# Two FFN-and-mixer blocks on one core: a bias table written from 128 partitions in four steps, a gain row spread by TensorE, smaller last parts

## Chip, cores and metric

One core of a Trainium2 chip runs the whole program in one launch. The metric is the device time in microseconds (us) of that core; the number that stands for a kernel is the median of its runs.

## The reference, cut

Two blocks of two layers each, over 256 tokens of width 1024 in float32; each layer is an FFN, a mixer and a second FFN of width 2816.

```python
def _rmsnorm(x, gain, eps=1e-6):
    return x * lax.rsqrt(jnp.mean(x * x, -1, keepdims=True) + eps) * gain
def _swiglu(h, w_gate, w_up, w_down):
    return (jax.nn.silu(h @ w_gate) * (h @ w_up)) @ w_down
...
# first block, layer l (the mixer is a convolution with RWKV-7 at l = 0, MLA attention at l = 1)
x = x + 0.5 * _swiglu(_rmsnorm(x, g[0]), ...)
x = x + mix(_rmsnorm(x, g[1]))
x = x + 0.5 * _swiglu(_rmsnorm(x, g[2]), ...)
...
# second block, layer l (the mixer is NSA attention at l = 0, HGRN-2 at l = 1), LN with mean, 1e-5
x = _layer_norm(alpha * x + 0.5 * _swiglu(x, ...), ln_gain[l, 0], ln_bias[l, 0])
x = _layer_norm(alpha * x + mix(x), ln_gain[l, 1], ln_bias[l, 1])
x = _layer_norm(alpha * x + 0.5 * _swiglu(x, ...), ln_gain[l, 2], ln_bias[l, 2])
...
def _rel_bias(table, dist):        # NSA: table is [32 buckets, 16 heads]
    return jnp.moveaxis(table[_t5_bucket(dist)], -1, 0)
```

## The kernel before

x stays in SBUF as two tiles of 128 tokens. Every float32 operand of a product is split into a high part, rounded to the type that TensorE multiplies fast, and a low part, the rest; a product is then three products, high by high, high by low and low by high. Weights are not kept: `weights` (L155) has SyncE load a piece of up to 128 x 2048 numbers, and `hi_lo` (L147) has ScalarE copy the high part (L152) and VectorE subtract the low part (L153), in two halves. Two sets of staging buffers, `st` and `xst`, and of split buffers, `sp` and `xsp`, are used in turn.

An FFN (`_ffn`, L341) walks over units of 256 hidden columns, 11 of them. A unit multiplies x, transposed as `xT`, by its gate and up columns into four rotating PSUM banks (`rot`); ScalarE and VectorE form silu(gate) * up and split it; the down product of the unit before is added to four accumulator banks (`acc`, `down`, L303, products at L181). The last three units' down products come at the end, for token tile 0 and then for token tile 1.

Each engine runs its instructions in one order that a scheduler lays out from the program; SyncE and GpSimd, and in the RWKV mixer ScalarE too (L677), issue DMAs. Work that a later mixer needs ahead of time waits in a list, `K.later`. From unit 4 of an FFN on, one entry of it is taken per unit, issued behind that unit's last multiplication and last activation:

```python
if self.later and u > 3:
    with self.behind_pow(), self.tc.issue_after(self.last_mul), self.tc.issue_after(self.last_act):
        self.later.pop(0)()
```

For NSA the entries are made by `nsa_setup` (L1205). A one-hot product makes the bias by relative distance, 16 heads (partitions) by 384 places, which VectorE copies to `bs` (L1221). It is then needed as `sk`, a DRAM tensor with 128 copies of that table, since the mixer reads it back skewed, each query row shifted by one place (`Gb`, L1280). Six entries, the function `piece`, write it, each 21 or 22 copies by one DMA of GpSimd's queue (L1227). Two further DRAM buffers of the RWKV mixer, `dT`, are filled with zeros by GpSimd's DMAs at the start (L515).

Norms are in `post` (L255). An RMS norm squares two halves with a running sum on ScalarE (L269), then GpSimd adds the halves (L271), multiplies and adds eps (L235) and raises to the power -0.5 (L236); VectorE multiplies x by it and by the gain (L278). Behind it the four halves are transposed on TensorE (L209) and copied and split into `xT` (L213, L214). A layer norm takes its sums with `bn_stats` and `bn_aggr` on VectorE, goes through the same two GpSimd steps, and ends with two VectorE passes (L290, L291). FFN results are added to x at L263.

The program starts (L1843) with SyncE loading x tile 0, then the first gain, spread over 128 partitions by the DMA (512 KB), then x tile 1, and the first weights.

Of the kernel before, what the change touches and what calls it, by code (L numbers as in the profile page):

```python
# [18 lines left out]
P = 128  # L19
# [41 lines left out]
class Core:  # L61
    def __init__(self, tc, ctx):
# [23 lines left out]
        self.second = None  # L86
        self.last_act = None
# [33 lines left out]


# [24 lines left out]
    def hi_lo(self, hi, lo, src):  # L147
# [7 lines left out]
    def weights(self, w, k0, nk, c0, ncols):  # L155
# [11 lines left out]
        self.hi_lo(hi[:, :m], lo[:, :m], st[:, :m])  # L167
        v = lambda a: a[:, :m].rearrange("p (k n) -> p k n", k=nk)
        return v(hi), v(lo)

    def mm3(self, out, terms, start, stop):
# [8 lines left out]
        for i, (a, b) in enumerate(seq):  # L180
            self.last_mm = nc.tensor.matmul(out, a, b, start=start and i == 0, stop=stop and i == n - 1).ins  # L181
# [22 lines left out]
    def transpose_split(self, src, xT, t, k0, nk=4, kind="rot"):  # L204
# [8 lines left out]
        nc.scalar.activation(hi, v, AF.Copy)  # L213
# [6 lines left out]
    def bcast(self, row, n=D, pool=None, tag="gain", bufs=None, queue=None):  # L220
# [8 lines left out]
        return g  # L229

# [24 lines left out]
    def post(self, t, acc, c, alpha=None, rms=None, ln=None, xT=None, out=None):  # L255
# [4 lines left out]
        if acc is not None:  # L260
            for h in range(2):
                s = slice(h * H, (h + 1) * H)
                nc.vector.scalar_tensor_tensor(x[:, s], acc[h], c, x[:, s], ALU.mult, ALU.add)  # L263
        src = [x[:, :H], x[:, H:]]
        if rms is not None:
            ss = self.tmp.tile([P, 4], F32, tag="ss", name=self.n("ss"))
            for h in range(2):
                junk = self.tmp.tile([P, H], F32, tag="xn", name=self.n("junk")) if acc else self.bank("acc")
                nc.scalar.activation(junk, x[:, h * H:(h + 1) * H], AF.Square, accum_out=ss[:, h:h + 1])  # L269
            with self.behind_pow():  # L270
                nc.gpsimd.tensor_tensor(ss[:, 2:3], ss[:, 0:1], ss[:, 1:2], ALU.add)  # L271
            self.rsqrt(ss[:, 3:4], ss[:, 2:3], 1.0 / D, 1e-6)
            yield
            src = []
            for h in range(2):
                s = slice(h * H, (h + 1) * H)
                xn = self.tmp.tile([P, H], F32, tag="xn", name=self.n("xn"))
                self.last_xn = nc.vector.scalar_tensor_tensor(xn, x[:, s], ss[:, 3:4], rms[:, s], ALU.mult, ALU.mult).ins  # L278
                src.append(xn)
            yield  # L280
        if ln is not None:
            st = self.tmp.tile([P, 2, 6], F32, tag="bn", name=self.n("bn"))
            for h in range(2):
                nc.vector.bn_stats(st[:, h, :], x[:, h * H:(h + 1) * H])  # L284
# [18 lines left out]
    def down(self, acc, yT, ws, first, last, toks=(0, 1), halves=(0, 1)):  # L303

        for t in toks:
            for j, (k0, wh, wl) in enumerate(ws):
                for h in halves:
                    s = slice(h * 512, (h + 1) * 512)
                    terms = [(yT[0][:, k0 + k, t * P:(t + 1) * P], yT[1][:, k0 + k, t * P:(t + 1) * P],
                              wh[:, k, s], wl[:, k, s]) for k in range(2)]  # L310
                    self.mm3(acc[t][h], terms, first and j == 0, last and j == len(ws) - 1)
# [21 lines left out]
    def ffn(self, xT, wg, wu, wd, mixed=False):  # L333

        with self.scoped("ff", 2) as self.ff:
# [3 lines left out]
            return self._ffn(xT, wg, wu, wd)  # L339

    def _ffn(self, xT, wg, wu, wd):  # L341
        nc = self.nc
        N = 256
        acc = self.new_acc()
# [49 lines left out]
        for u in range(first, NU):  # L394
# [3 lines left out]
            for w in (wg, wu):  # L398
# [28 lines left out]
        for t in range(2):  # L427
            for (v, y), w in zip(todo, ws):
                self.down(acc, y, [w], False, v == NU - 1, toks=(t,))
# [34 lines left out]
def rwkv_setup(K, p, w, consts):  # L464
# [47 lines left out]
    for s in range(2):  # L512
        ds = [K.dram.tile([8, ITEM], F32, name=f"{name}{s}") for name in ("dA", "dT")]
        for d in ds[1:]:
            nc.gpsimd.dma_start(d[:, :P * P].rearrange("i (p n) -> p i n", n=P),  # L515
                                z[:, :P].rearrange("p (o n) -> p o n", o=1).to_broadcast([P, 8, P]))
# [669 lines left out]
SKN = 6  # L1186
# [19 lines left out]
def nsa_setup(K, pc, w, consts):  # L1206
# [4 lines left out]
    with ExitStack() as ctx:  # L1211
        p = ctx.enter_context(scope)
        rel = p.tile([33, NH], F32, name="rel")
        nc.gpsimd.memset(rel, -1e30)
        nc.gpsimd.dma_start(rel[:32, :], w["rel_bias"])
# [3 lines left out]
        nc.tensor.matmul(bt[:NH, :LR], rel, oh, start=True, stop=True)  # L1219
        bs = p.tile([NH, LR], F32, name="bs")  # L1220
        nc.vector.tensor_copy(bs, bt[:NH, :LR])  # L1221
# [3 lines left out]
    def piece(r0, r1):  # L1225

        nc.gpsimd.dma_start(sk[r0:r1].rearrange("p h l -> h p l"), bs.rearrange("h (o l) -> h o l", o=1).to_broadcast([NH, r1 - r0, LR]))  # L1227
        if r1 == P:
            held.close()

    cuts = [P * n // SKN for n in range(SKN + 1)]
    K.later += [lambda a=a, b=b: piece(a, b) for a, b in zip(cuts, cuts[1:])]
# [593 lines left out]
def program(tc, i, out):  # L1826
    nc = tc.nc
    with ExitStack() as ctx:
# [37 lines left out]
        for l in range(2):  # L1866
# [6 lines left out]
            acc = K.ffn(xT, *ffn2(l, 1))  # L1873
            last = l == 1
            xT = K.after(acc, 0.5, alpha=alpha, ln=ln(l, 2), out=out[0] if last else None, keep_T=not last)
# [36 lines left out]
```

## Time and profile before

| what | value |
|---|---|
| runs shown | 2147.49, 2144.08 and 2138.15 us, median 2144.08 |
| the profiled execution | 2144.05 us, its span 2142.3 us |
| busy share of the span | TensorE 97%, weight loads 83%, VectorE 63%, ScalarE 51%, GpSimd 9% |
| mean granted TensorE clock | 0.992 of full speed |
| DMA | 367 MB, 171 GB/s as a mean over the span |
| first product of the first FFN | 14.62 us after the span's start |

The span is what the profiler saw between the first and the last instruction; the device time has 1.75 us around it. A busy share is a mean over the whole program, so a stretch in which another engine sets the pace shows only in a view of that stretch. A wait row names what the engine waited for last. In the timeline, "x8" means that eight like instructions in a row were joined, and the brackets hold the idle time ahead of them and what ended it. An engine whose name ends in q, as SPq, is issuing (here a DMA), and not computing. [...]

### The profile page before, as it was taken

The numbers are of one execution on the slowest core, as the hardware profiler recorded it, in microseconds if no ns is written. First come the engines' busy times: TensorE is split into PE (matmuls) and PEld (weight loads), VectorE is DVE, ScalarE is ACT, GpSimd is POOL, SyncE is SP. The second block draws the span as 40 slices with busy tenths as digits, with TensorE's granted clock in tenths as the row PEclk, the third lists the DMA queues.
The fourth block names the chain that finished last, engine by engine and source line by source line (L and its number), as shares of the span: only waits on it lengthen the run. The fifth ranks groups of instructions, "written<-read, shape, count | busy, mean of one in ns | idle before, by whom it ended". The sixth has DMA issues, their size and how long they took to land. (4 is left out here: it accounts for less than half of the span.)

```text
span 2142.3 us, 30750 instructions
## 1 busy us (share of the span) xinstructions
PE 2084.4 (97%) x12009; PEld 1788.2 (83%) x12009; DVE 1356.9 (63%) x2316; ACT 1103.1 (51%) x2032; POOL 192.1 (9%) x353
## 2 busy tenths in 40 slices
PE   8999999999999999999997999999999999999998
PEld 6888887788888887888886898788888888987887
DVE  5665764665566567656563667776666666766665
ACT  5554653555455556545453546645545555434553
POOL 2001050000100032000000010100010000241000
PEclk9999999999999999999999999999999999999999
DMA  9653433465566343765558564165546546326551
GB/s 308 213 181 101 130 117 124 169 215 196 169 208 203 131 139 109 250 214 180 156 197 177 188 192 143 41 215 190 190 152 243 185 149 209 126 80 236 189 191 53
DMA packets 257088, 367.27 MB, mean 171 GB/s; under 512 B 6945, under 2 KB 208293, under 8 KB 256944
## 3 DMA queue, kind: packets, MB, share of 16 engines
q1 hardware_dynamic: 249648, 348.48, 49.0%
q0 software_dynamic: 5184, 15.79, 3.4%
q8 instruction: 94, 1.54, 0.3%
q10 hardware_dynamic: 2112, 1.05, 0.2%
q14 instruction: 50, 0.41, 0.1%
HBM read 358.87 MB, written 6.42 MB: 171 GB/s over the span
## 5 line engine op out<-in xcount | busy, mean ns | idle before, releaser
L200 PE MATMUL rot<-xT,sp1h 128*128 128x512 f32 x784 | 196.7, 393 | 0.0
L200 PE MATMUL rot<-xT,sp0h 128*128 128x512 f32 x768 | 193.8, 394 | 1.3 <-DVE xT L214 1.3
L153 DVE TENSOR_TENSOR sp0l<-st,sp0h 128x1024 fp32r<-128x1024 f32 (+4 forms) x126 | 144.5, 1164 | 74.9 <-ACT sp0h L152 74.2
L365 ACT ACTIVATE g<-rot 128x256 f32<-128x256 f32 x296 | 103.9, 377 | 166.9 <-PE rot L202 166.9
L153 DVE TENSOR_TENSOR xsp0l<-xst,xsp0h 128x1024 fp32r<-128x1024 f32 (+4 forms) x106 | 116.9, 1128 | 87.4 <-ACT xsp0h L152 87.2
L366 DVE TENSOR_TENSOR g<-rot,g 128x256 f32<-128x256 f32 x296 | 117.9, 419 | 81.1 <-ACT g L365 80.9
L200 PEld LDWEIGHTS rot<-xT,sp0h 128*128 128x128 f32 x768 | 141.0, 190 | 28.7 <-DVE xT L214 1.7
L200 PEld LDWEIGHTS rot<-xT,sp1h 128*128 128x128 f32 x784 | 142.0, 189 | 26.5
L152 ACT ACTIVATE sp0h<-st 128x1024 fp32r<-128x1024 f32 (+4 forms) x126 | 123.6, 1003 | 62.1 <-PE acc L181 23.1
L153 DVE TENSOR_TENSOR xsp1l<-st,xsp1h 128x1024 fp32r<-128x1024 f32 x80 | 95.7, 1221 | 81.4 <-ACT xsp1h L152 81.4
L153 DVE TENSOR_TENSOR sp1l<-st,sp1h 128x1024 fp32r<-128x1024 f32 (+3 forms) x108 | 122.0, 1148 | 27.8 <-ACT sp1h L152 27.2
L152 ACT ACTIVATE xsp0h<-xst 128x1024 fp32r<-128x1024 f32 (+4 forms) x106 | 100.3, 979 | 70.9 <-DMA xst<-in_ffn_w_gate_dram 58.2
L153 DVE TENSOR_TENSOR sp1l<-xst,sp1h 128x1024 fp32r<-128x1024 f32 x80 | 95.8, 1222 | 60.0 <-ACT sp1h L152 60.0
L417 ACT ACTIVATE hTh<-h 128x256 fp32r<-128x256 f32 x148 | 61.7, 417 | 124.0 <-DVE h L359 124.0
L152 ACT ACTIVATE sp1h<-st 128x1024 fp32r<-128x1024 f32 (+3 forms) x108 | 104.3, 997 | 23.6 <-PE rot L181 7.4
L202 PEld LDWEIGHTS rot<-xT,sp1l 128*128 128x128 f32 x784 | 106.9, 190 | 7.7
L200 PE MATMUL rot<-xT,xsp1h 128*128 128x512 f32 x400 | 102.2, 398 | 10.9 <-ACT xsp1h L152 10.9
L202 PEld LDWEIGHTS rot<-xT,sp0l 128*128 128x128 f32 x768 | 105.0, 190 | 7.8
L152 ACT ACTIVATE xsp1h<-st 128x1024 fp32r<-128x1024 f32 x80 | 82.6, 1052 | 54.9 <-DMA st<-in_ffn_w_gate_dram 32.8
L202 PE MATMUL rot<-xT,sp1l 128*128 128x256 f32 x784 | 109.2, 282 | 0.0
L202 PE MATMUL rot<-xT,sp0l 128*128 128x256 f32 x768 | 107.2, 282 | 0.0
L200 PE MATMUL rot<-xT,xsp0h 128*128 128x512 f32 x416 | 104.6, 393 | 0.0
(570 smaller groups left out, 4922.8 us busy)
## 6 DMA issues: line engine op xcount, KB each, us to landing
st<-in_ffn_w_gate_dram SPq DMA_DIRECT2D x54, 1024.0 KB, 5.2
xst<-in_ffn_w_up_dram SPq DMA_DIRECT2D x48, 1024.0 KB, 5.9
xst<-in_ffn_w_down_dram SPq DMA_DIRECT2D x47, 1024.0 KB, 5.2
st<-in_ffn_w_down_dram SPq DMA_DIRECT2D x41, 1024.0 KB, 4.9
st<-in_ffn_w_up_dram SPq DMA_DIRECT2D x40, 1024.0 KB, 5.3
xst<-in_ffn_w_gate_dram SPq DMA_DIRECT2D x33, 1024.0 KB, 5.2
st<-in_even_w_in_dram SPq DMA_DIRECT2D x12, 1024.0 KB, 5.2
st<-in_hgrn_w_in_dram SPq DMA_DIRECT2D x8, 1024.0 KB, 5.4
```

Source lines behind the costliest of these rows:

```text
L152: self.nc.scalar.activation(hi[:, s], src[:, s], AF.Copy)
L153: self.nc.vector.tensor_sub(lo[:, s], src[:, s], hi[:, s].bitcast(F32))
L200: nc.tensor.matmul(b, wh, both.rearrange("p a n -> p (a n)"), start=i == 0, stop=False, skip_group_check=True)
L202: self.last_mm = nc.tensor.matmul(b[:, :T], wl, xh, start=False, stop=i == n - 1, skip_group_check=True).ins
L365: nc.scalar.activation(g, b[:, T:], AF.Copy)
L366: nc.vector.tensor_add(g, b[:, :T], g)
L417: nc.scalar.activation(y[0][:, i, :], h, AF.Copy)
```

## The change

It has five parts.

1. The bias table is formed on 128 partitions: the table of 16 heads is loaded eight times side by side, so that the one-hot product gives 8 x 16 rows. `sk` is then written by four DMAs of 128 x 4 x 384 numbers, on ScalarE's queue instead of GpSimd's. An empty entry goes ahead of them in `K.later`.
2. The two zero fills of `dT` go from the start of GpSimd's queue into `K.later`, on ScalarE's queue.
3. At the start, the first gain is loaded as one row of 4 KB, ahead of x. `start` issues 14 products of zeros on TensorE and two products of a row of ones by the gain row, which give the gain on all partitions in two accumulator banks, where L278 now reads it. x comes in four loads of 256 KB. The first gate unit's weight copies wait each for one tile's transposed copy (`last_T`) instead of the last normed half (`last_xn`).
4. The squares of an RMS norm are scaled by 1/32 (1/32 squared is 1/1024); eps is added to the first half's sum before the second is there; then come one add and the power. A layer norm's eps is added by VectorE instead of GpSimd.
5. In the last FFN the products of token tile 1 go by output halves, and the very last piece of the second half in two quarters of 256 columns; the final `post` adds the result for that tile in three parts and takes four `bn_stats` of 256.

```diff
+    def start(self, row):
+        nc = self.nc
+        ones = self.gain.tile([P, D], F32, tag="gain", name="ones")[:1, :P]
+        nc.gpsimd.memset(ones, 1.0)
+        idle = self.bank("rot")
+        for _ in range(8):
+            self.zero_bank(idle)
+        out = []
+        for h in range(2):
+            b = self.bank("acc")
+            nc.tensor.matmul(b, ones, row[:, h * 512:(h + 1) * 512], start=True, stop=True)
+            out.append(b)
+        for _ in range(6):
+            self.zero_bank(idle)
+        return out
...
-            self.nc.scalar.activation(hi[:, s], src[:, s], AF.Copy)
+            with self.tc.issue_after(behind[i]) if behind else ExitStack():
+                self.nc.scalar.activation(hi[:, s], src[:, s], AF.Copy)
...
+    def rsqrt_of(self, out, src):
+        self.last_pow = self.nc.gpsimd.tensor_tensor(out, src, self.mhalf, ALU.pow).ins
...
     def post(...)
-            for h in range(2):
-                s = slice(h * H, (h + 1) * H)
-                nc.vector.scalar_tensor_tensor(x[:, s], acc[h], c, x[:, s], ALU.mult, ALU.add)
+            cuts = (0, H, D) if out is None or t == 0 else (0, H, H + H // 2, D)
+            for a, b in zip(cuts, cuts[1:]):
+                s = slice(a, b)
+                nc.vector.scalar_tensor_tensor(x[:, s], acc[a // H][:, a % H:a % H + b - a], c, x[:, s], ...)
...
-                nc.scalar.activation(junk, x[:, h * H:(h + 1) * H], AF.Square, accum_out=ss[:, h:h + 1])
-            with self.behind_pow():
-                nc.gpsimd.tensor_tensor(ss[:, 2:3], ss[:, 0:1], ss[:, 1:2], ALU.add)
-            self.rsqrt(ss[:, 3:4], ss[:, 2:3], 1.0 / D, 1e-6)
+                nc.scalar.activation(junk, x[:, h * H:(h + 1) * H], AF.Square, scale=1.0 / 32, accum_out=...)
+                if h == 0:
+                    with self.behind_pow():
+                        nc.gpsimd.tensor_scalar(ss[:, 2:3], ss[:, 0:1], 1.0, 1e-6, ALU.mult, ALU.add)
+            nc.gpsimd.tensor_tensor(ss[:, 3:4], ss[:, 1:2], ss[:, 2:3], ALU.add)
+            self.rsqrt_of(ss[:, 3:4], ss[:, 3:4])
...
-            self.rsqrt(mv[:, 2:3], mv[:, 1:2], 1.0, 1e-5)
+            nc.vector.tensor_scalar(mv[:, 2:3], mv[:, 1:2], 1e-5, None, ALU.add)
+            self.rsqrt_of(mv[:, 2:3], mv[:, 2:3])
...
     _ffn(...)
-                    with self.tc.issue_after(self.last_xn):
-                        wh, wl = unit(w, u)
+                    wh, wl = self.weights(w, 0, KD, 0, N, behind=self.last_T)
...
+            if not (end and t):
+                for (v, y), w in zip(todo, ws):
+                    self.down(acc, y, [w], False, v == NU - 1, toks=(t,))
+                continue
+            for h in range(2):
+                for (v, y), w in zip(todo, ws):
+                    for q in (range(2) if h and v == NU - 1 else (None,)):
+                        self.down(acc, y, [w], False, v == NU - 1, toks=(t,), halves=(h,), quarter=q)
...
-            nc.gpsimd.dma_start(d[:, :P * P]...)
+        K.later.append(lambda d=ds[1]: nc.scalar.dma_start(d[:, :P * P]...))
...
     nsa_setup
-        rel = p.tile([33, NH], F32, name="rel")
+        rel = p.tile([33, 8, NH], F32, name="rel")
...
-        nc.tensor.matmul(bt[:NH, :LR], rel, oh, start=True, stop=True)
+        nc.tensor.matmul(bt[:, :LR], rel.rearrange("b r h -> b (r h)"), oh, start=True, stop=True)
...
-        nc.gpsimd.dma_start(sk[r0:r1].rearrange("p h l -> h p l"), bs...to_broadcast([NH, r1 - r0, LR]))
+        m = P // 8 // SKN
+        v = sk.rearrange("(k r) h l -> (r h) k l", r=8)[:, n * m:(n + 1) * m, :]
+        nc.scalar.dma_start(v, bs.to_broadcast([P, m, LR]))
...
+    K.later += [lambda: None] + [lambda n=n: piece(n) for n in range(SKN)]
...
     program
-        nc.sync.dma_start(K.x[0], i["x"][0, :P, :])
-        g0 = K.bcast(gains[0, 0], queue=nc.sync)
-        nc.sync.dma_start(K.x[1], i["x"][0, P:, :])
+        nc.sync.dma_start(row, gains[0, 0].rearrange("(o n) -> o n", o=1))
+        for t in range(2):
+            for h in range(2):
+                s = slice(h * 512, (h + 1) * 512)
+                nc.sync.dma_start(K.x[t][:, s], i["x"][0, t * P:(t + 1) * P, s])
+        g0 = K.start(row)
```

The scheduler decides where the instructions land. GpSimd, the FFN ahead of NSA, before (`cw` is a weight of the mixer, `sk` the DRAM table, `mv` the next norm's sums):

```order
L1238 DMA cw_10382<-in_nsa_cmp_w_2_dram 128x2x64
L1227 DMA sk<-bs 16x21x384 x2
L1227 DMA sk<-bs 16x22x384
L1227 DMA sk<-bs 16x21x384 x2
L1227 DMA sk<-bs 16x22x384
L235 TENSOR_SCALAR mv_11319<-mv_11319 128x1
L236 TENSOR_TENSOR mv_11319<-mv_11319,mhalf 128x1
```

The same stretch of GpSimd with the change:

```order
L1275 DMA crow<-in_c_crow_dram 128x1
L1277 DMA cpos<-in_nsa_cmp_pos_dram 128x32x1
L1279 DMA cw_10405<-in_nsa_cmp_w_2_dram 128x2x64
L253 TENSOR_TENSOR mv_11340<-mv_11340,mhalf 128x1
L1327 MEMSET vcb 128x1024
```

The six writes are gone from GpSimd, and of the norm's two steps one is left. ScalarE in that FFN before, about one unit of it (L152 are weight copies, L365, L354 and L417 the steps from the gate's product to the split hidden values):

```order
L365 ACTIVATE g_10650<-rot_10609 128x256
L365 ACTIVATE g_10657<-rot_10584 128x256
L354 ACTIVATE s_10660<-g_10657 128x256
L417 ACTIVATE hTh_10643<-h_10653 128x256
L152 ACTIVATE sp0h_10746<-st_1797_10744 128x1024
L365 ACTIVATE g_10662<-rot_10626 128x256
L152 ACTIVATE sp0h_10746<-st_1797_10744 128x1024
L417 ACTIVATE hTh_10643<-h_10665 128x256
L152 ACTIVATE sp1h_10815<-xst_1812_10813 128x1024 x2
```

ScalarE there with the change, from behind the first bias write to the second (L172 are the weight copies now, L400, L389 and L451 the other steps; one row further ahead stands the first write, `L1269 DMA sk<-bs 128x4x384`):

```order
L451 ACTIVATE hTh_10665<-h_10675 128x256
L400 ACTIVATE g_10684<-rot_10648 128x256
L172 ACTIVATE sp0h_10768<-st_1799_10766 128x1024 x2
L451 ACTIVATE hTh_10665<-h_10687 128x256
L172 ACTIVATE sp1h_10837<-xst_1814_10835 128x1024 x2
L400 ACTIVATE g_10810<-rot_10732 128x256
L389 ACTIVATE s_10813<-g_10810 128x256
L172 ACTIVATE xsp1h_10911<-st_1822_10909 128x1024 x2
L400 ACTIVATE g_10815<-rot_10774 128x256
L400 ACTIVATE g_10822<-rot_10749 128x256
L389 ACTIVATE s_10825<-g_10822 128x256
L1269 DMA sk<-bs 128x4x384
```

Each write stands behind the last activation of one unit, 12 rows from the next. TensorE at the start of the program, before (L209 are the transposes, of which twelve more stand ahead of these, and nothing else; L200 and L202 are the first products):

```order
L209 MATMUL rot_139<-ident,xn_116 128x128 x4
L200 MATMUL rot_165<-xT_93,sp0h_159 128x512 x8
L202 MATMUL rot_165<-xT_93,sp0l_160 128x256 x4
L200 MATMUL rot_182<-xT_93,sp0h_159 128x512 x3
L202 MATMUL rot_165<-xT_93,sp0l_160 128x256 x4
```

TensorE there with the change (L229 are the transposes):

```order
L122 LDWEIGHTS zero
L122 MATMUL rot_97<-zero 128x512
L135 MATMUL acc_106<-row,ones 128x512
L135 MATMUL acc_108<-row,ones 128x512
L229 MATMUL rot_141<-ident,xn_133 128x128 x4
```

All 14 products of zeros stand ahead of the two that spread the gain row, the last of them in the first two rows here; behind the two stand the transposes, as before.

## Rows read from the trace of the kernel before

**Rows 1.** Waits of TensorE: what ended them, us, count, longest.

```profile
PE rot L200 <- ACT xsp1h L152: 10.9, 1, 10.9
...
PE rot L181 <- ACT xT L213: 3.8, 13, 0.8
```

**Rows 2.** The bias table `sk`: its writes' issue, then landing, us.

```profile
L1227 POOL DMA_DIRECT2D sk<-bs x6: 596/596/639, 1132.5 to 1135.5; - x6
...
DMA to landing us min/median/max: 8.4/19.1/32.2
```

**Rows 3.** Windows: us, busy PE, PEld, DVE, ACT, POOL, PEclk, DMA share, GB/s.

```profile
1140.00:1145.00 5.00, 5.00 (x31) 4.44 (x30) 3.31 (x6) 2.72 (x7) 0.00 (x0) 1.00 0.95 99
...
1170.00:1175.00 5.00, 0.00 (x0) 0.00 (x0) 0.00 (x0) 0.23 (x1) 0.00 (x0) 0.70 0.63 221
...
1175.00:1180.00 5.00, 1.96 (x5) 1.57 (x6) 4.14 (x5) 4.79 (x8) 0.00 (x0) 0.50 0.07 10
```

**Rows 4.** Timeline 1147 to 1186: start, duration, instruction [idle before <-releaser].

```profile
1147.74 9.27 SPq L165 DMA_DIRECT2D xst<-in_ffn_w_gate_dram  x1
...
1166.54 0.63 PE L181 MATMUL acc<-sp1h,hTl 128*128 128x512 f32 x2
...
1174.77 1.06 ACT L152 ACTIVATE xsp0h<-xst 128x1024 fp32r<-128x1024 f32 x1 [26.27 <-DMA xst<-in_ffn_w_gate_dram]
...
1178.04 3.78 PE L200 MATMUL rot<-xT,xsp1h 128*128 128x512 f32 x8 [10.88 <-ACT xsp1h L152]
...
1182.84 2.03 PE L200 MATMUL rot<-xT,xsp1h 128*128 128x512 f32 x8
```

**Rows 5.** Page, DMA issues: count, KB each, median us to landing.

```profile
xst<-in_ffn_w_gate_dram SPq DMA_DIRECT2D x33, 1024.0 KB, 5.2
```

**Rows 6.** Chain that ended last, 2028 to 2047: start, us, step.

```profile
2028.34 1.81 PE rot L200 x8
...
2031.11 1.84 PE rot L200 x8
...
2044.95 1.81 PE rot L200 x8
```

**Rows 7.** Timeline from 0 to 19.

```profile
0.86 0.53 POOL L92 MEMSET zero<- 128x512 bf16 x1
...
1.17 0.42 SPq L225 DMA_DIRECT2D gain<-in_norm_gains_dram  x1
...
4.71 0.60 ACT L269 ACTIVATE acc<-x 128x512 f32<-128x512 f32 x1 [2.71 <-DMA x<-in_x_dram]
...
5.25 0.19 ACT L269 ACTIVATION_READ_ACCUMULATOR acc<-x 128x1 f32 x1
...
6.65 0.20 POOL L235 TENSOR_SCALAR ss<-ss 128x1 f32<-128x1 f32 x1
...
6.93 0.56 POOL L236 TENSOR_TENSOR ss<-ss,mhalf 128x1 f32<-128x1 f32 x1
...
7.92 0.60 ACT L269 ACTIVATE acc<-x 128x512 f32<-128x512 f32 x1 [1.88 <-DMA x<-in_x_dram]
...
10.52 1.41 DVE L278 SCALAR_TENSOR_TENSOR xn<-x,ss,gain 128x512 f32<-128x512 f32 x2 [1.58 <-POOL ss L236]
...
14.62 3.78 PE L200 MATMUL rot<-xT,sp0h 128*128 128x512 f32 x8 [1.32 <-DVE xT L214]
```

**Rows 8.** Groups of TensorE by shape: busy us, mean ns | idle before.

```profile
L586 PE MATMUL acc<-low,wa 32*128 32x256 f32 x16 | 5.6, 426 | 0.0
```

**Rows 9.** Timeline 2126 to 2143, the end.

```profile
2132.85 0.61 PE L181 MATMUL acc<-xsp1h,hTl 128*128 128x512 f32 x2
...
2132.97 0.68 DVE L263 SCALAR_TENSOR_TENSOR x<-acc,x 128x512 f32<-128x512 f32 x1
...
2136.03 0.75 POOL L235 TENSOR_SCALAR mv<-mv 128x1 f32<-128x1 f32 x1 [4.43 <-DVE mv L286]
```

**Rows 10.** DMAs that ScalarE issues, line 677: min/median/max ns, when.

```profile
L677 ACTq DMA_DIRECT2D dA<-A x4: 366/367/382, 264.1 to 301.6; - x4
```

More of the change, by code (lines that the diff above doesn't have):

```diff
@@ L145, in split_w, with hi_lo @@
         return hi, lo
-    def hi_lo(self, hi, lo, src):
+    def hi_lo(self, hi, lo, src, behind=None):
         n = src.shape[-1] // self.parts
@@ L166, in weights, with mm3 @@
         hi, lo = self.split_w()
-        self.hi_lo(hi[:, :m], lo[:, :m], st[:, :m])
+        self.hi_lo(hi[:, :m], lo[:, :m], st[:, :m], behind)
         v = lambda a: a[:, :m].rearrange("p (k n) -> p k n", k=nk)
         return v(hi), v(lo)
-    def mm3(self, out, terms, start, stop):
+    def mm3(self, out, terms, start, stop, **k):
         nc = self.nc
@@ L180, in mm3 @@
         for i, (a, b) in enumerate(seq):
-            self.last_mm = nc.tensor.matmul(out, a, b, start=start and i == 0, stop=stop and i == n - 1).ins
+            self.last_mm = nc.tensor.matmul(out, a, b, start=start and i == 0, stop=stop and i == n - 1, **k).ins
     def mm3_steps(self, out, terms, step=8):
@@ L281, in post @@
         if ln is not None:
-            st = self.tmp.tile([P, 2, 6], F32, tag="bn", name=self.n("bn"))
-            for h in range(2):
-                nc.vector.bn_stats(st[:, h, :], x[:, h * H:(h + 1) * H])
+            st = self.tmp.tile([P, 4, 6], F32, tag="bn", name=self.n("bn"))
+            if out is None or t == 0:
+                st = st[:, :2]
+            n = D // st.shape[1]
+            for h in range(st.shape[1]):
+                nc.vector.bn_stats(st[:, h, :], x[:, h * n:(h + 1) * n])
             mv = self.tmp.tile([P, 4], F32, tag="mv", name=self.n("mv"))
             nc.vector.bn_aggr(mv[:, 0:2], st)
-            self.rsqrt(mv[:, 2:3], mv[:, 1:2], 1.0, 1e-5)
+            nc.vector.tensor_scalar(mv[:, 2:3], mv[:, 1:2], 1e-5, None, ALU.add)
+            self.rsqrt_of(mv[:, 2:3], mv[:, 2:3])
             for h in range(2):
@@ L301, in new_acc, with down @@
         return [[self.bank("acc") for _ in range(2)] for _ in range(2)]
-    def down(self, acc, yT, ws, first, last, toks=(0, 1), halves=(0, 1)):
+    def down(self, acc, yT, ws, first, last, toks=(0, 1), halves=(0, 1), quarter=None):
         for t in toks:
@@ L307, in down @@
                 for h in halves:
-                    s = slice(h * 512, (h + 1) * 512)
+                    o = slice(0, 512) if quarter is None else slice(quarter * 256, quarter * 256 + 256)
+                    s = slice(h * 512 + o.start, h * 512 + o.stop)
                     terms = [(yT[0][:, k0 + k, t * P:(t + 1) * P], yT[1][:, k0 + k, t * P:(t + 1) * P],
                               wh[:, k, s], wl[:, k, s]) for k in range(2)]
-                    self.mm3(acc[t][h], terms, first and j == 0, last and j == len(ws) - 1)
+                    self.mm3(acc[t][h][:, o], terms, first and j == 0, last and j == len(ws) - 1,
+                             **({"skip_group_check": True} if self.loose else {}))
     def out_proj(self, yT, w, tail=2):
@@ L331, in out_steps, with ffn @@
             self.down(acc, yT, held, tail == 4, True)
[L333 removed]
+    def ffn(self, xT, wg, wu, wd, mixed=False, end=False):
         with self.scoped("ff", 2) as self.ff:
@@ L1872, in program @@
             xT = K.after(acc, 1.0, alpha=alpha, ln=ln(l, 1))
-            acc = K.ffn(xT, *ffn2(l, 1))
             last = l == 1
+            acc = K.ffn(xT, *ffn2(l, 1), end=last)
             xT = K.after(acc, 0.5, alpha=alpha, ln=ln(l, 2), out=out[0] if last else None, keep_T=not last)
```

40 lines of the change are left out of this document (20 added, 20 removed).

## Prediction

> **What bounds the kernel now.** I read the waits of TensorE first: nearly all of its work is back to back, so only its idle stretches and what stands before its first and after its last product can be won. The list of waits has one long entry, 10.9 us in a single wait on ScalarE's copy of a gate weight, and far smaller ones, of which those on the normed and transposed x have 3.8 us in all [rows 1]. So I looked at three places: the stretch around the long wait, the start, and the end.
>
> **The long wait** lies in the FFN ahead of the NSA mixer. The six writes of the bias table are issued by GpSimd within 3.6 us at 1132.5, and land 8.4 to 32.2 us later, the last at about 1135.5 + 32.2 = 1167.7 [rows 2]. Meanwhile the DMA engines are nearly fully occupied (0.95 of the time) and move only 99 GB/s [rows 3]. SyncE's load of a gate weight at 1147.74 takes 9.27 us to be issued and reaches ScalarE at 1174.77; ScalarE runs in order, so the copy that TensorE needs next stands behind that one. [...]
>
> **The change, part by part.**
>
> *Bias table.* The order of ScalarE shows the four new writes 12 rows apart, one in each FFN unit, where GpSimd had all six in a row with nothing between them. A unit lasts 2044.95 - 2028.34 = 16.6 us [rows 6]. Each write is 128 x 4 x 384 x 4 bytes = 768 KB. What has to be known is how late a gate load may be. The late one took 1174.77 - 1147.74 = 27.0 us [rows 4]; the same kind of load takes 5.2 us as a median of 33 [rows 5]. It was 21.8 us late and TensorE stood for 10.9, so 10.9 us of lateness are covered. A write of 768 KB at the old pace (128 x 16 x 384 x 4 bytes, 3072 KB, from 1132.5 to 1167.7, 87 KB per us [rows 2]) lasts 8.8 us. Even a load that waited out a whole write would be inside the cover, and 16.6 us lie between two writes. So the wait goes, with the slow products behind it: the next pair of product groups came 1182.84 - 1178.04 = 4.80 us after the first [rows 4], against 2031.11 - 2028.34 = 2.77 us [rows 6]. **Term A = 10.9 + 2.0 = 12.9 us.** Bounds: 6.4 (half remains) and 12.9.
>
> [...] What the trace shows is 99 GB/s at an occupancy of 0.95 while 16 partitions are read [rows 3]. [...]
>
> Forming the table on 128 partitions changes neither the columns of the one product nor the length of the one VectorE copy: nothing. ScalarE issues six more DMAs, two of them the zero fills that leave GpSimd's start. The one kind of DMA that ScalarE issues today costs it 0.37 us [rows 10]; ScalarE is idle half of the time, and the copies ahead of a unit absorb that: nothing, and if the cover were gone, 6 x 0.37 = 2.2 us. The fills' 1 MB move from a start in which the DMA is full to units 5 and 6, under the same cover of 10.9 us.
>
> *Start.* Today the x tile reaches ScalarE at 4.71, the second at 7.92, with the 512 KB gain between them: about 1.6 us per 512 KB. The power ends at 7.49, the four normed halves at 11.93, and the first product starts at 14.62 [rows 7]. In the change a 4 KB row goes first and x comes in halves of 256 KB, 0.8 us each. The first half should land at 4.71 + 0.42 (one more issue, [rows 7]) - 0.8 = 4.33, the last at 6.73. Each square needs 0.60 and the reading of its sum 0.19 [rows 7], then come an add of 0.2 and the power (0.56): ready at 6.9 and 8.4 for the two tiles. But the gain now comes out of TensorE, behind 14 products of zeros. They can start at 1.4, when the zero tile is written [rows 7], at 3.78 / 8 = 0.47 us each or less [rows 4]: they end between 6.4 (if the clock comes up part of the way, as it did between the first and the next products behind the long wait) and 7.4 to 8.0. The two products that spread the row are plain f32 over 512 columns; a 256-column one takes 0.43 us at full clock [rows 8], so 0.85 each, or 1.7 at half. The gain's second half is there at 8.1 at best and 11.4 at worst. VectorE's four normed halves then end at 10.3 to 13.5, against 11.93. I take 10.8: it is nearest to the case where the clock has risen, since the zeros are dense. ScalarE now puts its first weight copy (1.06) between the two tiles' copies, some of it on the path, so of 1.1 us I count **0.9** at the first product.
>
> The clock is the other half of the start. The first eight products took 3.78 us [rows 7], the same as behind the long wait, where 2.0 us were lost. If the zeros bring the clock up and it stays up until the first product, at about 13.5, those 2.0 us come back. **Term B = 0.9 + 2.0 = 2.9 us**, bounds -1.6 (gain late, clock low) and 4.5. Behind the first unit the weights must not become the limit: the start is full of DMA, but 0.5 MB of gain and 1 MB of fills leave it, some 4.8 us at 1.6 us per 512 KB, more than TensorE gains.
>
> [...] The sixteen transposes that stand between the power and the first product of today's start did not raise the clock: the products behind them take 3.78 us [rows 7]. [...]
>
> *Norms.* An RMS norm loses one GpSimd step of 0.20 us between square sum and power [rows 7], a layer norm has a GpSimd step of 0.75 us [rows 9] done by VectorE in an estimated 0.1 to 0.2. TensorE waits for all such copies 3.8 us in the whole kernel, 0.8 at the longest [rows 1], since other products cover the chain. **Term C = 0.2 us**, bounds 0 and 2.
>
> *End.* The last products end at 2133.46, but VectorE takes up the second tile only at 2132.97, because the first tile's norm holds it until then [rows 9]; from there it is VectorE and GpSimd to the end. So cutting the last products into quarters releases nothing early. What helps is the GpSimd step of 0.75 that leaves both chains; three more VectorE instructions and the step itself cost back most of it. **Term D = 0.3 us**, bounds -0.4 and 1.5.
>
> **Sum:** 12.9 + 2.9 + 0.2 + 0.3 = 16.3 us. The profiled execution took 2144.05 us (span 2142.3, 1.75 around it), the median of the runs is 2144.08; the prediction is 2144.05 - 16.3 = **2127.8 us**.
>
> **Rivals.**
> 1. *The clock is low at the first product.* For it: the sixteen transposes of today leave the clock low [rows 7], and 4 to 5 us lie between the spread row (8.1 to 9.8) and the first product (13.5). Against: in the long wait, which began at 1167.17, the clock did not fall at once: from 1170 to 1175, with no product at all, the granted clock still reads 0.70, between its two levels [rows 3]. Price 2.0: 2129.8. Chance 0.27.
> 2. *The spread row is late.* TensorE takes the 14 zeros first, at half clock throughout; the normed halves end 1.6 us later than today, and the start loses instead of gaining, though the clock is up then: term B near 0.4, 2130.3; with the clock low as well -1.6, 2132.3. Chance 0.12.
> 3. *Half of the long wait stays,* because a spread write and two weight loads together make one load later than 10.9 us. For it: under the six writes the weights' loads had to share the 99 GB/s [rows 3]. Against: 8.8 < 10.9. Price 6.4: 2134.2. Chance 0.06.
> 4. *The writes don't spread.* If ScalarE ran ahead they would bunch as before: A = 0, 2140.7. Against: each stands behind an activation that needs the same unit's products. Chance 0.02.
> 5. *Slower: the issue blocks ScalarE.* SyncE needed 9.27 us for one issue when its queue was backed up [rows 4]. If the four writes and two fills did this to ScalarE, its evictions would stop, and TensorE with them once its four rotating banks are full. It can go on for 2044.95 - 2031.11 = 13.8 us (three more banks and the down products, [rows 6]). A block of 9.27 costs nothing; the change is slower only if a block exceeds 13.8 + 16.3 / 6 = 16.5 us. At 19.1, the median landing of today's writes [rows 2], six would cost 31.8 us: 2159.6. Against: ScalarE's own queue is empty, and its issues take 0.37 [rows 10]. Chance 0.03.
>
> **How the numbers follow.** Forecast 0.50, rivals as above. The range runs from 2120, every bound at its best (12.9 + 4.5 + 2 + 1.5 = 20.9, so 2123) with 3 us for the spread of the runs shown, to 2136, rival 3 with the end's worst bound and a little of that spread; rivals 4 and 5 are left out. About what a measurement of this kernel can tell from no change is 0.5%, 10.7 us. Faster than 2133.4: the forecast and rivals 1 and 2, 0.89, less 0.03 for scatter: 0.86. Same: 0.11. Slower: 0.03.
>
> **What the new profile would show.** Term A: no wait over 2 us of TensorE on ScalarE's weight copies, four bias writes some 16 us apart on ScalarE's queue, weight copies never waiting for a load for 20 us. Term B: spread row done by 8 to 9 us, first product at 13 to 14, its eight in about 2.0 us. Term D: no GpSimd step ahead of the last power. The prediction is wrong if a wait of over 5 us stands anywhere in that FFN, or if the start's first unit ends no earlier than today.

## The result, and the profile after

The changed kernel takes 2122.94 us (median of four runs, 2122.35 to 2123.18) against 2142.81 of the kernel before beside it: a ratio of 0.991, interval 0.9895 to 0.9924, 19.9 us less. The prediction was 2127.8 us, 16.3 less, in a range that holds the result. The profiled execution has a span of 2120.6 us against 2142.3, 21.7 less; TensorE's busy time is the same (2084.3 and 2084.4 us), but after the change it holds 7.3 us of zeros and gain spread at the start. So all other products took about 7 us less, and the other 14 us of the gain are waiting that went.

The waits of TensorE after, the first rows of the list:

```profile
PE acc L1105 <- DVE qs L1094: 4.3, 3, 2.2
PE rot L201 <- ACT xT L233: 4.2, 15, 0.8
PE rot L229 <- DVE o L1823: 2.6, 4, 0.8
```

The wait of 10.9 us [rows 1] is gone. Next the bias table's writes, with their landings, and windows of 5 us behind the first write (columns as in [rows 3]):

```profile
L1269 ACTq DMA_DIRECT2D sk<-bs x4: 366/366/367, 1154.1 to 1204.5; - x4
...
DMA to landing us min/median/max: 5.9/6.0/8.5
```

```profile
1155.00:1160.00 5.00, 5.00 (x26) 4.13 (x25) 3.89 (x6) 2.58 (x4) 0.00 (x0) 1.00 1.03 316
1160.00:1165.00 5.00, 5.00 (x27) 4.19 (x26) 2.67 (x3) 2.40 (x3) 0.00 (x0) 1.00 0.80 272
```

Issue costs ScalarE 0.37 us, a write lands in 6 us where the old ones took 8.4 to 32.2 [rows 2], and busy DMA engines now move 316 GB/s where they moved 99 [rows 3]. The start after, from its timeline:

```profile
1.45 5.30 PE L122 MATMUL rot<-zero 128*128 128x512 bf16 x14 [1.45 <-POOL zero L94]
5.72 0.56 POOL L253 TENSOR_TENSOR ss<-ss,mhalf 128x1 f32<-128x1 f32 x1
6.67 1.98 PE L135 MATMUL acc<-row,ones 1*128 1x512 f32 x4
6.78 0.60 ACT L295 ACTIVATE rot<-x 128x512 f32<-128x512 f32 x1
7.90 1.54 DVE L306 SCALAR_TENSOR_TENSOR xn<-x,ss,acc 128x512 f32<-128x512 f32 x2 [7.90 <-POOL ss L299]
13.52 2.10 PE L220 MATMUL rot<-xT,sp0h 128*128 128x512 f32 x8 [0.82 <-DVE xT L234]
```

The zeros and the spread end at 8.65. The first normed half waits for the first of the two spread products (its power is done at 6.28), and the first eight products start 1.1 us earlier and take 2.10 us instead of 3.78 [rows 7].

To place the rest, each product of one trace was paired with the same product of the other, and the difference of their starts read at the ends of stages; the table has what each stage gained on the kernel before, in us, good to about 0.1. The other columns are experiments told below; of the kernel before there is one profile.

| stage (us of the trace before) | changed | changed, again | old bias table | old LN eps | old end |
|---|---|---|---|---|---|
| start, first products (to 24) | 2.8 | 0.9 | 2.9 | 2.8 | 3.5 |
| to the end of FFN 3 (760) | 0.6 | -0.6 | -0.8 | -1.0 | 1.3 |
| MLA (to 860) | 2.5 | 2.9 | 3.2 | 3.1 | 2.3 |
| next FFN (to 1100) | 0.1 | -0.1 | -0.1 | -0.1 | -0.2 |
| FFN ahead of NSA (to 1215) | 13.1 | 13.2 | 1.0 | 13.1 | 13.1 |
| NSA, next FFN (to 1570) | 0.1 | -1.5 | 0.0 | 0.6 | 0.0 |
| layer norm (to 1612) | 1.0 | 0.9 | 1.0 | 0.1 | 1.0 |
| FFN (to 1770) | 0.0 | 0.1 | 0.0 | 0.0 | 0.0 |
| layer norms around HGRN (to 1965) | 1.1 | 1.8 | 1.4 | 0.2 | 2.0 |
| last FFN (to 2100) | -0.5 | -0.5 | -0.4 | -0.5 | -0.5 |
| end | 0.9 | 0.9 | 0.6 | -0.1 | 1.0 |
| sum | 21.7 | 18.0 | 8.8 | 18.2 | 23.5 |

### The profile page after: what moved, and what is told of

Its sections match the earlier page's. It is cut to its first block, busy times and chain, and to the rows that moved or that the text cites. A ratio compares the mean times of both kernels' runs of the same rounds, so it can differ in the third digit from the quotient of the medians.

```text
span 2120.6 us, 30815 instructions
## 1 busy us (share of the span) xinstructions
PE 2084.3 (98%) x12033; PEld 1781.6 (84%) x12033; DVE 1357.7 (64%) x2331; ACT 1104.3 (52%) x2032; POOL 179.0 (8%) x334
## 5 line engine op out<-in xcount | busy, mean ns | idle before, releaser
L400 ACT ACTIVATE g<-rot 128x256 f32<-128x256 f32 x296 | 104.0, 377 | 183.5 <-PE rot L222 183.5
L172 ACT ACTIVATE sp0h<-st 128x1024 fp32r<-128x1024 f32 (+4 forms) x126 | 123.4, 1004 | 66.9 <-PE acc L201 26.3
L172 ACT ACTIVATE xsp0h<-xst 128x1024 fp32r<-128x1024 f32 (+4 forms) x106 | 100.2, 979 | 44.9 <-DMA xst<-in_ffn_w_gate_dram 27.6
L451 ACT ACTIVATE hTh<-h 128x256 fp32r<-128x256 f32 x148 | 61.6, 416 | 113.5 <-DVE h L394 113.5
L172 ACT ACTIVATE sp1h<-st 128x1024 fp32r<-128x1024 f32 (+3 forms) x108 | 104.3, 997 | 21.6 <-PE rot L201 7.4
L172 ACT ACTIVATE xsp1h<-st 128x1024 fp32r<-128x1024 f32 x80 | 82.5, 1053 | 54.6 <-DMA st<-in_ffn_w_gate_dram 31.1
```

What stands on the lines that cost most here:

```text
L400: nc.scalar.activation(g, b[:, T:], AF.Copy)
L451: nc.scalar.activation(y[0][:, i, :], h, AF.Copy)
```

## Experiments

Each is the changed kernel with one edit. Runs of the first four share a chip, as do the next four and the three after them.

**The old bias table back** (16 partitions, six writes on GpSimd's queue).

```diff
-        nc.tensor.matmul(bt[:, :LR], rel.rearrange("b r h -> b (r h)"), oh, start=True, stop=True)
+        nc.tensor.matmul(bt[:NH, :LR], rel, oh, start=True, stop=True)
...
-        nc.scalar.dma_start(v, bs.to_broadcast([P, m, LR]))
+        nc.gpsimd.dma_start(sk[r0:r1].rearrange("p h l -> h p l"), bs...to_broadcast([NH, r1 - r0, LR]))
```

> The changed kernel with the bias table of before (16 partitions, six writes on GpSimd's queue); all other parts stay. If the table is the whole of the gain in the FFN ahead of NSA, the wait of about 11 us comes back with the slow products behind it: 13 us slower than the changed kernel, near 2136. If a good part of the 20 us came from the other parts, or from chance in the granted clock, it is 6 us or less.

2135.21 us, ratio to the kernel before 0.9969 (0.9956 to 0.9981). The FFN ahead of NSA loses all but 1.0 of its 13.1 us, and ScalarE's longest wait for a gate load there is 25.3 us, as before (26.27, [rows 4]). TensorE's long wait is back:

```profile
PE rot L220 <- ACT xsp1h L172: 10.0, 1, 10.0
```

So 12.1 of the 13.1 us in that stage are the table's. This run differs from the changed kernel in width, queue, spacing and number of the writes at once; three runs below take these apart.

**The old start back.**

```diff
-        g0 = K.start(row)
+        g0 = K.bcast(gains[0, 0], queue=nc.sync)
...
-                    wh, wl = self.weights(w, 0, KD, 0, N, behind=self.last_T)
+                    with self.tc.issue_after(self.last_xn):
+                        wh, wl = unit(w, u)
```

> The changed kernel with the start of before: gain spread by the DMA, x in two loads, no products of zeros. Aligned product by product, the two traces differ by 1.1 us at the first product and by 2.8 us after the first eight. Theory: 2.8 us slower, near 2125.7, first product near 14 with half clock behind it. Rival: the first weights set the pace of the first units, so that most of it is given back within them: less than 1 us slower.

2130.04 us, ratio 0.9944 (0.9931 to 0.9957). The profile, of its fastest run (2126.76), is 2.2 us behind the changed kernel at 22 us and 1.9 at 370, so hardly anything is given back within the first units. Its first product comes at 14.37, 0.25 ahead of the kernel before, and it gains 0.6 on that kernel by 24 us: so much of the stage's 2.8 is not of this edit. The rest of its distance came behind 1250, where no edit is, so the medians can't price the start alone.

**The layer norm's eps back on GpSimd.**

```diff
-            nc.vector.tensor_scalar(mv[:, 2:3], mv[:, 1:2], 1e-5, None, ALU.add)
-            self.rsqrt_of(mv[:, 2:3], mv[:, 2:3])
+            self.rsqrt(mv[:, 2:3], mv[:, 1:2], 1.0, 1e-5)
```

> The changed kernel with a layer norm's eps added by GpSimd again. The prediction put all norms at 0.2 us. New theory: VectorE's last pass waits for GpSimd, and weight splits that TensorE needs stand behind it, about 0.8 us at each of three norms, and 0.5 to 0.75 at the very end: 2.5 to 3.5 us slower, near 2125.5. By the prediction's reasoning (other products cover the chain): under 1 us.

2129.76 us, ratio 0.9933 (0.992 to 0.9947). Paired with the changed kernel it loses 1.0, 0.2 and 0.7 us at three norms (ahead of HGRN, and two around it) and 0.9 at the end: 2.8. At the second of the three the changed kernel's own profile lost 0.3 to 0.9 us that no other run lost; against the changed kernel again, the loss there is 1.0. The timeline of this run at the norm ahead of HGRN, where the first two rows are the two GpSimd steps:

```profile
1584.12 0.75 POOL L259 TENSOR_SCALAR mv<-mv 128x1 f32<-128x1 f32 x1 [5.37 <-DVE mv L317]
1584.95 0.94 POOL L260 TENSOR_TENSOR mv<-mv,mhalf 128x1 f32<-128x1 f32 x1
1585.92 0.75 DVE L322 SCALAR_TENSOR_TENSOR x<-x,mv,gain 128x512 f32<-128x512 f32 x1 [0.44 <-POOL mv L260]
1586.59 2.35 DVE L173 TENSOR_TENSOR xsp0l<-xst,xsp0h 128x1024 fp32r<-128x1024 f32 x2
1587.86 0.50 PE L201 MATMUL rot<-xsp0l,xT 128*128 128x512 f32 x1 [0.42 <-DVE xsp0l L173]
```

The same place in the changed kernel:

```profile
1583.21 0.92 POOL L253 TENSOR_TENSOR mv<-mv,mhalf 128x1 f32<-128x1 f32 x1 [5.73 <-DVE mv L318]
1584.31 0.74 DVE L323 SCALAR_TENSOR_TENSOR x<-x,mv,gain 128x512 f32<-128x512 f32 x1
1584.97 2.35 DVE L173 TENSOR_TENSOR xsp0l<-xst,xsp0h 128x1024 fp32r<-128x1024 f32 x2
1586.24 0.50 PE L201 MATMUL rot<-xsp0l,xT 128*128 128x512 f32 x1
```

VectorE waits 0.44 us for the longer GpSimd chain, and a weight split stands behind it in VectorE's order; TensorE waits for that split, not for x. In the changed kernel VectorE does not wait.

**The old end back** (old order of the last products, halves, two statistics).

```diff
-            acc = K.ffn(xT, *ffn2(l, 1), end=last)
+            acc = K.ffn(xT, *ffn2(l, 1), end=False)
-            cuts = (0, H, D) if out is None or t == 0 else (0, H, H + H // 2, D)
+            cuts = (0, H, D)
```

> The changed kernel without its last part: the last FFN's down products in the old order, the sum into x in halves and two statistics of 512 for both tiles. The prediction holds that VectorE sets the end and that the cut releases nothing: within 0.4 us of the changed kernel. Rival: the earlier first half lets VectorE start on the second tile sooner: 1 us or more slower without it.

2124.74 us, ratio 0.9919 (0.9906 to 0.9933). Its end gains 1.0 us against 0.9: in its one profile the cut is worth nothing, and VectorE sets the end either way: the chain that ended last is VectorE's alone from 2108.03 on here (span 2118.8) and from 2109.73 on in the changed kernel (span 2120.6).

**Four writes from 128 partitions on GpSimd's queue.**

```diff
-        nc.scalar.dma_start(v, bs.to_broadcast([P, m, LR]))
+        nc.gpsimd.dma_start(v, bs.to_broadcast([P, m, LR]))
```

> The changed kernel with its four bias writes from 128 partitions on GpSimd's queue, where nothing spaces them. If the spacing by ScalarE's order is what removed the wait, the four writes go out together and a wait of 5 to 11 us returns. If the width of the source alone is enough (each write landing in a few us), no wait over 2 us returns and the time stays within 1 us of the changed kernel.

2126.62 us, ratio 0.9915 (0.9902 to 0.9929). All four go out together, yet the FFN ahead of NSA keeps its gain (the run is 2.6 us behind the changed kernel ahead of that FFN, and 2.6 behind it). Issue and landings, then the window:

```profile
L1269 POOL DMA_DIRECT2D sk<-bs x4: 752/756/788, 1128.0 to 1130.2; - x4
...
DMA to landing us min/median/max: 5.8/9.0/10.9
```

```profile
1133.00:1138.00 5.00, 5.00 (x30) 4.33 (x29) 3.06 (x4) 2.82 (x4) 0.00 (x0) 1.00 1.01 387
```

The whole table is written within 13.1 us (1128.0 to 1130.2 + 10.9 at the latest) at up to 387 GB/s with the weights beside it. So this run did without the spacing, and GpSimd's queue was not what made the old writes late.

**Four writes from 16 partitions, one per unit, on ScalarE's queue.**

```diff
-        nc.tensor.matmul(bt[:, :LR], rel.rearrange("b r h -> b (r h)"), oh, start=True, stop=True)
+        nc.tensor.matmul(bt[:NH, :LR], rel, oh, start=True, stop=True)
...
-        nc.scalar.dma_start(v, bs.to_broadcast([P, m, LR]))
+        nc.scalar.dma_start(sk[r0:r1].rearrange("p h l -> h p l"), bs...to_broadcast([NH, r1 - r0, LR]))
```

> The changed kernel with the table on 16 partitions, but written in four steps on ScalarE's queue, one per unit. By the prediction a write of 768 KB at the old pace takes 8.8 us and is covered: within 1 us of the changed kernel, landings near 9 us. Rival: the narrow source slows the weight loads that run beside it so much that a gate load is late by more than the cover: 2 us or more slower in that FFN.

2130.38 us, ratio 0.993 (0.9918 to 0.9943). The four writes land in (first row), and the two windows behind the first of them are:

```profile
DMA to landing us min/median/max: 9.6/9.9/10.1
...
1155.00:1160.00 5.00, 5.00 (x27) 4.23 (x26) 3.66 (x6) 3.34 (x6) 0.00 (x0) 1.00 1.06 357
1160.00:1165.00 5.00, 5.00 (x27) 4.18 (x26) 0.56 (x2) 0.03 (x1) 0.00 (x0) 1.00 0.96 189
```

That is a little over the 8.8 us of the prediction, and the FFN keeps its gain (13.2 us by the same pairing). The windows also show that one write from 16 partitions beside the weight loads does not hold the sum at 99 GB/s, as the six at once did. The run loses 6 us later, at the norm ahead of NSA, for another reason: the scheduler put two weight copies ahead of ScalarE's `xT` copies, and ScalarE waited there 7.28 us for their load. That load was issued only at 1230.3, 13 us after the last write had landed (1206.9 + 10.1), so the loss is of this kernel's order and says nothing of the writes.

**Four writes from 128 partitions in one unit, on ScalarE's queue.**

```diff
-    K.later += [lambda: None] + [lambda n=n: piece(n) for n in range(SKN)]
+    K.later += [lambda: None, lambda: [piece(n) for n in range(SKN)]]
```

> The changed kernel with all four writes from 128 partitions in one entry of the list, on ScalarE's queue within one unit. By the pace of the single writes of the changed kernel (5.9 to 8.5 us each) four in a row would take up to 30 us and make a gate load late: 3 to 10 us slower. If the pace of a single write is set by the loads beside it and not by the write, the four take less and the cover of 10.9 us holds: within 1 us.

2124.07 us, ratio 0.9907 (0.9894 to 0.9921), nothing lost in that FFN (the run is 4.3 us behind the changed kernel both ahead of it and behind it); the longest landing is 9.9 us. One issue took ScalarE 1.86 us, the others 0.37. So all four were written within 13.3 us (1158.3 to 1161.7 + 9.9 at the latest), not in up to 30.

**The RMS norm's old steps back.**

```diff
-                nc.scalar.activation(junk, x[:, h * H:(h + 1) * H], AF.Square, scale=1.0 / 32, accum_out=...)
+                nc.scalar.activation(junk, x[:, h * H:(h + 1) * H], AF.Square, accum_out=...)
...
-            self.rsqrt_of(ss[:, 3:4], ss[:, 3:4])
+            self.rsqrt(ss[:, 3:4], ss[:, 2:3], 1.0 / D, 1e-6)
```

> The changed kernel with the RMS norm's GpSimd steps of before (add, multiply and add, power). Prediction: 0.2 us or less. Aligned traces show 1.0 us gained at the norm behind the first mixer (before: 384 to 390 us) and some at the start: by that 1 to 1.5 us slower. If it is under 0.4 us, that place moved for another reason, such as the granted clock.

2126.95 us, ratio 0.991 (0.9895 to 0.9926): the time of the run with GpSimd's queue beside it. It is 1.9 us behind the changed kernel at the norm behind the first mixer, but so are the kernels with the old eps of the layer norm (1.7) and with the four writes in one unit (1.9), which keep the new RMS steps. At the start its first product comes at 13.76, between the 13.52 and 13.96 of the changed kernel's two profiles. So no place shows a price of the old steps, and in sum it is under the scatter.

**The changed kernel again, on another chip.**

> The changed kernel itself on another chip. In its profile the clock was low for a moment in four places besides the end (at 9, 381, 794 and 1320 us). If what the mixers gained there (about 2.2 us in MLA and 1.2 us in NSA against the kernel before) comes from the change, this run is the same at these places within 0.3 us; if it is the chance of where the clock falls, it differs there by 0.5 to 2 us, and the time by as much.

2125.38 us, ratio 0.9911 (0.9897 to 0.9924). Its profile is 3.7 us longer than the first one, and differs at the start and behind the first mixer by up to 2 us, in NSA by 1.6 and in MLA by 0.4 (table), with no edit. For NSA that speaks for chance; for MLA it is too little to tell. But there three windows of the kernel before, of the changed kernel and of the run with four writes in one unit, whose MLA is the changed kernel's, do:

```profile
785.00:790.00 5.00, 4.60 (x19) 4.05 (x20) 4.06 (x15) 1.43 (x4) 2.54 (x6) 0.66 0.00 0
...
795.00:800.00 5.00, 3.29 (x12) 2.45 (x13) 3.32 (x11) 2.88 (x11) 3.29 (x7) 0.65 0.62 210
800.00:805.00 5.00, 5.00 (x18) 3.94 (x17) 3.09 (x13) 2.31 (x8) 1.53 (x4) 0.67 0.64 210
```

```profile
785.00:790.00 5.00, 4.84 (x25) 3.83 (x24) 3.47 (x8) 3.72 (x14) 0.49 (x1) 1.00 0.00 0
790.00:795.00 5.00, 2.56 (x13) 2.08 (x14) 3.57 (x11) 3.88 (x14) 3.16 (x8) 0.92 0.54 211
795.00:800.00 5.00, 5.00 (x21) 3.88 (x21) 2.74 (x13) 1.89 (x7) 2.05 (x4) 0.74 0.64 210
```

```profile
784.00:789.00 5.00, 5.00 (x22) 4.46 (x23) 3.95 (x14) 1.43 (x4) 2.19 (x4) 0.66 0.00 0
...
794.00:799.00 5.00, 3.77 (x13) 2.92 (x14) 3.76 (x11) 2.88 (x10) 3.28 (x7) 0.61 0.67 212
799.00:804.00 5.00, 5.00 (x20) 3.77 (x19) 2.64 (x12) 1.84 (x7) 1.04 (x3) 0.71 0.51 203
```

The granted clock (1.00 is full speed) is low in the same pattern before (0.66, 0.65, 0.67) and in the third kernel (0.66, 0.61, 0.71), which runs the changed code there, and higher in the second. Of the thirteen profiles with the changed code in MLA, ten gain 2.3 to 3.2 us there, but this third kernel gains 0.4, and the next two kernels below gain 0.35 and 0.2. So the 2.5 us come with the clock of the execution and not with every run of the changed code; as there is one profile of the kernel before, whether the change makes the higher clock likelier stays open.

**No zeros,** and **the spread ahead of most of them** (4 zeros, spread, 6 zeros).

```diff
-        for _ in range(8):
-            self.zero_bank(idle)
...
-        for _ in range(6):
-            self.zero_bank(idle)
```

> The changed kernel without its 14 products of zeros. If the zeros only delay the spread row, the first product comes about 1 us earlier (near 12.5). If they bring the clock up for the first products, the first eight take about 3.8 us again in every profile instead of 2.1: net 0.5 to 1 us slower than the changed kernel.

```diff
-        for _ in range(8):
+        for _ in range(4):
...
...
+            with self.tc.issue_after(last):
+                self.zero_bank(idle)
```

(`last` is the second product of the spread.)

> The changed kernel with 4 products of zeros, then the spread of the row, then 6 more of zeros. The changed kernel's first normed half waited for the spread until 7.90 us, though its power was done at 6.28. Theory: normed halves and first product 1 to 1.5 us earlier (near 12.3), clock up: 1 us faster. Rival: the spread products at half clock take over 3 us and end as late as before: no difference.

2131.57 us, ratio 0.9943 (0.9929 to 0.9956), and 2134.47 us, ratio 0.995 (0.9938 to 0.9963): both far slower, for a reason that neither theory had. Two rows of ScalarE's timeline in the second:

```profile
13.84 2.00 ACT L173 ACTIVATE sp1h<-st 128x1024 fp32r<-128x1024 f32 x2 [5.47 <-DMA st<-in_ffn_w_up_dram]
15.74 1.06 ACT L234 ACTIVATE xT<-rot 128x512 fp32r<-128x512 f32 x2
```

The copies of the up weights, which nothing holds back, were laid ahead of the `xT` copies, and ScalarE waited for their load; the first product came at 19.46 (17.60 without zeros). What the zeros are worth can't be read from the times of these two.

**The same spread, with the up weights' copies held behind the second tile's `xT` copy.**

```diff
+                elif first == u == 0:
+                    wh, wl = self.weights(w, 0, KD, 0, N, behind=[self.last_T[1]] * 2)
```

> The spread ahead of most of the zeros, as in the run before it, but with the copies of the first up weights held behind the second tile's transposed copy, so that ScalarE's order is that of the changed kernel. In the run before, the normed half began at 7.07 us against 7.90 to 8.48, and everything after was lost to ScalarE waiting for the up weights. Theory: first product near 12.8 (the changed kernel: 12.5 to 14.0), 0.5 to 1 us faster than the changed kernel where the clock is alike, 2 us slower where the clock is low for the first eight products. Rival: the second tile's x sets the first product, and it stays at 13.5.

2124.90 us, ratio 0.9913 (0.9899 to 0.9926), the same as the changed kernel. Its first normed half starts at 7.30, 0.6 us earlier than the changed kernel's, but the first product not before 14.02:

```profile
8.66 0.60 ACT L296 ACTIVATE rot<-x 128x512 f32<-128x512 f32 x1 [1.16 <-DMA x<-in_x_dram]
9.80 0.56 POOL L254 TENSOR_TENSOR ss<-ss,mhalf 128x1 f32<-128x1 f32 x1
14.02 3.65 PE L221 MATMUL rot<-xT,sp0h 128*128 128x512 f32 x8 [1.24 <-DVE xT L235]
```

The last half of x reached ScalarE at 8.66 (6.78 in the changed kernel's profile) and the second tile's power ended at 10.36. The rival holds for this run: x's second tile sets the first product.

## Why the prediction was right, and where it was not

**Term A** (12.9 us): right in size, 13.1 to 13.2 us in every run that has the wide table, 1.0 with the old one. Its reason was half of it. The prediction let the spacing of the writes carry the gain, at the old pace of 8.8 us a write. The runs show two remedies, each enough alone: a wide source without spacing, and spacing with the old narrow source (9.6 to 10.1 us a write, near what was worked out). Where several writes were under way, the DMA engines moved 99 GB/s with six narrow ones and up to 387 with four wide ones on GpSimd's queue; with a single narrow one it was 357 and 189. Beside the weight loads a wide write landed in 6.0 us (the median of four). The 99 GB/s of the prediction is of writes and loads together; the writes alone moved 87 KB per us [rows 2]. Four narrow writes at once were not run, so width and number are not fully parted. Rivals 3, 4 and 5 did not come: no wait over 2.2 us, writes 16.8 us apart, issues of 0.37 us. Rival 5's 19.1 us also counts a later read of the table; the six writes alone have a median of 20.8, which changes that rival's price only.

**Term B** (2.9 us): 2.8 us in the first profile, 0.9 in the second, and 0.8 to 3.8 over the eight profiles that have the changed start and the new RMS steps. The 1.1 us at the first product, taken as 0.9, was right in size, but not by its steps. The last normed half ended at 11.46 (10.71 + 0.75) and not at 10.8, and the first product followed it sooner than before, by 2.06 us against 2.69. The powers, for which the prediction's steps add up to 6.7 and 8.3 and not to its 6.9 and 8.4, ended at 6.28 and 8.48. The loads of x (0.8 us each, the last at 6.73) held in two of four profiles with all 14 zeros ahead of the spread (ScalarE took up the last half at 6.78 in the changed kernel and 6.94 with the spaced narrow writes); with the old end it came at 7.83 and in the changed kernel again at 8.10.

The clock half is rival 1's, and it is a matter of the execution. Of the nine profiles with all 14 zeros ahead of the spread, six show the first eight products at 2.1 us and three at 3.6 to 3.8 (the four writes on GpSimd's queue, the old RMS steps, and the changed kernel again, whose row is this):

```profile
13.96 3.57 PE L220 MATMUL rot<-xT,sp0h 128*128 128x512 f32 x8 [0.82 <-DVE xT L234]
```

In all four kernels without zeros or with other zeros the first products were slow, as before (3.78 for eight): 3.42 us for eight with the old start, 4.21 for nine without zeros, 5.06 for eleven with the spread ahead, 3.65 for eight with the copies held. In the kernel before and with the old start the granted clock reads 1.00 from 1 to 22 us all the same: what the prediction calls a low clock in the start of before is read from the time of the products alone. So 0.27 for rival 1 was about right. But "stays up until the first product" is the step that held in two profiles only, the old end and the spaced narrow writes, where the granted clock reads 1.00 from 7 to 16 us. In the other four of the six, the changed kernel's first among them, it fell while the transposes ran, as rival 1 had it, and was back just in time (columns: us, TensorE busy, granted clock, DMA share, GB/s):

```profile
7.00:10.00 3.00, 2.83 (x10) 0.86 1.06 363
10.00:13.00 3.00, 2.69 (x12) 0.57 1.10 352
13.00:16.00 3.00, 2.48 (x13) 1.00 1.12 344
```

So that the first profile met the 2.9 is partly luck.

**Term C** (0.2 us) is the step that failed. VectorE's step for eps took what was estimated (0.15 us in the changed kernel); the waits were misread. "TensorE waits for all such copies 3.8 us, 0.8 at the longest" looked only at waits on x. The list of before has further rows, of which the first is the start's and belongs to term B:

```profile
PE rot L209 <- DVE xn L278: 9.4, 2, 8.3
...
PE rot L181 <- DVE xsp0l L153: 1.9, 4, 0.7
```

The second is of waits on VectorE's low parts of weights. Three of its four, 0.4, 0.7 and 0.5 us, lie at the layer norms ahead of HGRN and around it, where VectorE stood in the norm for GpSimd. In the changed kernel the row is gone, and with the old eps it is back:

```profile
PE rot L201 <- DVE xsp0l L173: 1.6, 3, 0.7
```

By the table, moving eps off GpSimd was worth 0.9 us at the first of these norms and 0.9 to 1.8 around HGRN, 1.8 to 2.7 us in all. The RMS norms' part stays open, too small to separate.

**Term D** (0.3 us) came to 0.9 us. That the cut releases nothing was right (1.0 without it). But the GpSimd step was not given back: with it VectorE waited 0.44 and 0.46 us on the two tiles, without it not at all, and the old eps alone takes the end's gain away.

**The sum.** In the first profile the four parts make 13.1 + 2.8 + 2.1 + 0.9 = 18.9 of the 21.7 us, in the second 13.2 + 0.9 + 2.7 + 0.9 = 17.7 of 18.0; the medians on the two chips gained 19.9 and 18.1, against 16.3 predicted. What the first profile has beyond its parts is mostly MLA's 2.5, of the clock; in the second, MLA's 2.9 is nearly used up by losses in other stages. About 0.5 us is lost in the last FFN in every column. Most of it lies in three units: in the run with the old eps, 24 down products in a row take 5.59 to 5.60 us there, where each unit took 5.47 before. Why stays open.

## What to carry to other kernels

When a norm's chain crosses engines, look for what stands behind its last step on the waiting engine: the price can show up as waits of TensorE on something else, here on weights (0.4 to 0.7 us each). Writes that made weight loads late, and TensorE wait 10.9 us, were cured here either by a wider source or by spacing them; try one at a time, to know which was needed. Where a scheduler lays the order out, an edit at the start can put a copy that waits for a load ahead of the ones on the path (here the first product came at 19.46 and 17.60 us instead of 13.52), and every such copy wants a written constraint.

## What was not expected of the hardware

In the changed kernel's first profile the granted clock falls at four places: at 9 us (0.57 from 10 to 13), 381 (0.66 from 380 to 385), 794 (0.74 from 795 to 800) and 1320 (0.67 from 1320 to 1325). In its second profile the third of these comes sooner: 0.82 and 0.84 from 782 to 792, where the first reads 1.00 up to 790. The time of one kernel moves with it: the runs of the second chip's changed kernel took 2126.06, 2126.83, 2124.70 and 2120.64 us at mean granted clocks of 0.993, 0.993, 0.994 and 0.997, 6.2 us between the extremes. An edit worth 1 to 3 us can't be told from this by medians of five runs; pairing the products of two traces, place by place, can where the granted clock reads alike in both.
